# Gate and up of the second feed-forward as seven products of half blocks, with its input scaled in place and the last four output blocks of the merge in one group

## The chip, the cores and the metric

The kernel runs on one core of one Trainium2 chip. The metric is the device time in microseconds (us) of one execution; lower is better. TensorE (PE) does the matmuls and writes to PSUM, which has eight banks. VectorE (DVE), ScalarE (ACT) and GpSimd (POOL) do the work between them, and SyncE (SP) issues nearly all transfers. Each engine takes its instructions in the order in which they stand in its own queue; semaphores tie the queues together.

## What is computed

One step of a hybrid streaming encoder over 1072 rows: 16 meta tokens, 1024 prompt frames, 32 sample frames. The parts that matter here, cut from the reference:

```python
def half_ffn(x, g, w_gate, w_up, w_down):
    h = rmsnorm(x, g)
    return x + 0.5 * ((jax.nn.silu(h @ w_gate) * (h @ w_up)) @ w_down)

x = half_ffn(x, ffn1...)            # first feed-forward, D_MODEL 1024, D_FF 2816
...                                 # projections, attention branch oa, recurrent branch ob
merged = gates[..., :D_MODEL] * (oa @ w_branch_a) + gates[..., D_MODEL:] * (ob @ w_branch_b)
x = x + merged @ w_out
x = half_ffn(x, ffn2...)            # second feed-forward
y = rmsnorm(x, final_norm)
```

The meta rows are not part of the output, so that everything from the merge on runs over 1056 columns.

## The kernel before, in words

Activations lie transposed: model channels on the partitions (8 blocks of 128), rows of the batch along the free axis. Every operand is split into a high part (`h`, rounded to fp32r) and a low part (`l`, the rest); a product of two operands is three matmuls, high by high, high by low, low by high. A split is one ACT copy and one DVE subtraction (`split`, and `weights` for a weight block of 128x1024: `whi` by ACT L184, `wlo` by DVE L185). Three `whi`/`wlo` buffers rotate, and two raw buffers into which SP loads.

The **first feed-forward** cuts the 1072 columns into four blocks of 268 and works in three stages. `first_units(0)` and `first_units(1)` compute the first two of 22 column blocks of gate and up in the plain way: per quarter `q` and matrix 24 matmuls of 268 columns. Between them DVE and ACT form the sums of half blocks `T1` to `T4` (`sums`). Then ten rounds of `unit` for gate and for up compute two column blocks at once with seven products of half blocks (12 matmuls each, for each of two column halves `b`) where the plain way has eight. DVE forms the sums of weights for it (`sa`, `sb`). The middle results go to `mid_dram`. Last, `mid` loads and splits them, and the down products run, 6 matmuls for each of 8 output blocks `m` and three column tiles, added into `acc` by DVE.

The **merge** runs over the column tiles `TD`, which are called A (384 columns from 16), B (384 from 400) and C (288 from 784) below. `merge(m)` makes one of eight blocks of `merged`; `out_block` multiplies two of them by `w_out` and DVE adds the result to `acc` (L1381). The order is merge 0, 1, 2, out(0,1), merge 3, 4, out(2,3), merge 5, 6, out(4,5), merge 7, out(6,7).

The **second feed-forward** (`ffn`) has no sums. `scaled`/`normalise` splits `acc` times the gain into `xh2`, `xl2` as soon as a tile of `acc` is final (ACT L216, DVE L217); this does not need the norm. Beside it the squares are summed over the 8 blocks: five blocks on POOL, three on DVE. `finish` then multiplies the sums by a matrix of ones on PE, and `scale_rows` makes the row factor `R2` from that: three ACT steps and four POOL steps (L249 to L252). `R2` is used only behind the products, in `finish` of `gate_up` (L284, L286). Each of 22 column blocks needs 24 matmuls for each matrix and tile; after every second block, two blocks of down products run. The last two are followed by the final norm (`after2`).

A tile framework puts each engine's instructions into an order of its own when the kernel is built, by its own costs; `PE.on` holds PE to the order in which the code is written.

## Time and profile before

| what | value |
|---|---|
| median of 3 runs | 2548.09 us (2545.7 to 2548.61) |
| the profiled execution | 2547.18 us, its span 2545.4 us |
| PE busy in the span | 2497.2 us (98%) |
| DVE, ACT, POOL busy | 1418.6, 815.5, 247.0 us |
| merge to second feed-forward, 1755 to 1800 us | PE busy 43.08 of 45 us |
| second feed-forward, 1800 to 2540 us | PE busy 735.84 of 740 us |
| units of the first feed-forward, 113 to 505 us | PE busy 392.00 of 392 us |

"Busy" of PE counts overlapping matmuls once. An idle stretch is shown in brackets behind the instruction that ended it, with the engine that released it. A matmul's printed duration (0.34 us) includes its passage through the array; the pace of a stream is the distance from start to start.

### The profile page before, as it was taken

What the parts mean: (1) busy time and instruction counts of PE and PEld (TensorE: products, weight loads), DVE (VectorE), ACT (ScalarE), POOL (GpSimd) and SP (SyncE); (2) the same over time, 40 slices, a digit from 0 to 9 for tenths busy, and PEclk for the clock granted to TensorE, in tenths of its full rate; (3) what the DMA queues carried; (4) which work ended last, traced back from release to release, by engine and by line L of the source; (5) the groups of instructions that cost most, each with busy time, mean ns of one, the idle gap of its engine ahead of it and who ended that gap; (6) DMA issues with size and microseconds to landing.
All of it is one profiled execution on the core that took longest, in us unless ns stands there. A gap on an engine that the chain in (4) does not pass through costs nothing.

```text
span 2545.4 us, 44180 instructions
## 1 busy us (share of the span) xinstructions
PE 2497.2 (98%) x18396; PEld 2397.6 (94%) x18396; DVE 1418.6 (56%) x2635; ACT 815.5 (32%) x1652; POOL 247.0 (10%) x388
## 2 busy tenths in 40 slices
PE   6999999999999999999999999999999999999998
PEld 5999999999998999998888888999999999999998
DVE  4655555577675467764655665557443444444445
ACT  6433333411124233332544543325211111111113
POOL 1000000000003012221000000214111001000100
PEclk9999999999999999999999999999999999999999
DMA  7122222352222111112111214321111111111112
GB/s 200 58 88 68 85 68 90 109 185 84 87 73 90 42 43 55 47 58 59 43 47 43 68 52 150 119 84 42 51 50 38 46 50 50 37 48 50 49 35 77
DMA packets 219182, 179.38 MB, mean 70 GB/s; under 512 B 37270, under 2 KB 202390, under 8 KB 218982
## 3 DMA queue, kind: packets, MB, share of 16 engines
q1 hardware_dynamic: 218950, 176.56, 22.3%
q8 instruction: 144, 2.36, 0.4%
q14 instruction: 56, 0.46, 0.1%
q0 software_dynamic: 32, 0.00, 0.0%
HBM read 137.78 MB, written 38.75 MB: 69 GB/s over the span
## 4 chain that ended last, share of the span: by engine, by line
PE 92%; DVE 5%; ACT 2%; issue 1%; DMA 1%; POOL 0%; SPq 0%; DVEq 0%; ACTq 0%; POOLq 0%
PE ps_z L100 37%; PE ps_mm L100 33%; PE ps_o L100 11%; PE ps_tr L100 8%; PE ps_tr L103 2%; DVE xl L217 1%; PE ps_z L103 1%; DVE wlo L185 1%; ACT whi L184 0%; PE ps_mm L103 0%; DVE left L993 0%; DVE acc L1381 0%; DMA xt<-in_x_prompt_dram 0%; DMA ga<-gate_dram 0%; DVE sd L875 0%
## 5 line engine op out<-in xcount | busy, mean ns | idle before, releaser
L100 PE MATMUL ps_mm<-xh,whi 128*128 128x384 f32 (+2 forms) x1224 | 405.4, 331 | 0.5 <-DVE raw L1201 0.5
L100 PE MATMUL ps_mm<-xh,wlo 128*128 128x384 f32 (+2 forms) x1224 | 399.1, 326 | 0.0
L100 PE MATMUL ps_mm<-xl,whi 128*128 128x384 f32 (+2 forms) x1224 | 398.2, 325 | 0.0
L184 ACT ACTIVATE whi<-raw 128x1024 fp32r<-128x1024 f32 x152 | 158.1, 1056 | 669.5 <-PE ps_z L100 429.4
L100 PEld LDWEIGHTS ps_mm<-xh,whi 128*128 128x128 f32 x1224 | 230.5, 188 | 9.1 <-issue 5.0
L100 PE MATMUL ps_z<-xh,whi 128*128 128x384 f32 (+2 forms) x720 | 234.9, 326 | 4.0 <-ACT whi L184 2.4
L100 PE MATMUL ps_z<-xh,wlo 128*128 128x384 f32 (+2 forms) x720 | 234.0, 325 | 0.1
L100 PE MATMUL ps_z<-xl,whi 128*128 128x384 f32 (+2 forms) x720 | 234.0, 325 | 0.0
L100 PEld LDWEIGHTS ps_mm<-xl,whi 128*128 128x128 f32 x1224 | 230.5, 188 | 1.2
L100 PEld LDWEIGHTS ps_mm<-xh,wlo 128*128 128x128 f32 x1224 | 230.7, 189 | 0.4
L185 DVE TENSOR_TENSOR wlo<-raw,whi 128x1024 fp32r<-128x1024 f32 x152 | 185.8, 1236 | 46.6 <-ACT whi L184 44.1
L100 PEld LDWEIGHTS ps_z<-xh,whi 128*128 128x128 f32 x720 | 136.1, 189 | 5.0 <-ACT whi L184 2.7
L286 POOL TENSOR_TENSOR g<-g,R 128x384 f32<-128x384 f32 (+1 forms) x66 | 77.7, 1178 | 641.4 <-ACT g L116 641.4
L993 DVE TENSOR_TENSOR_SCAN left<-left,oneb 128x512 f32<-128x512 f32 (+6 forms) x112 | 107.3, 958 | 54.8 <-ACT left L116 54.2
L100 PEld LDWEIGHTS ps_z<-xh,wlo 128*128 128x128 f32 x720 | 136.5, 190 | 0.9 <-DVE wlo L185 0.9
L100 PEld LDWEIGHTS ps_z<-xl,whi 128*128 128x128 f32 x720 | 136.2, 189 | 0.2
L287 DVE TENSOR_TENSOR g<-ps_z,g 128x384 f32<-128x384 f32 (+1 forms) x66 | 34.6, 524 | 179.1 <-PE ps_z L100 177.9
L116 ACT ACTIVATE g<-g 128x268 f32<-128x268 f32 (+2 forms) x126 | 58.1, 461 | 192.5 <-DVE g L284 148.3
L100 PE MATMUL ps_z<-ml,whi 128*128 128x384 f32 (+1 forms) x360 | 116.4, 323 | 0.0
L100 PE MATMUL ps_z<-mh,wlo 128*128 128x384 f32 (+1 forms) x360 | 115.8, 322 | 0.0
L100 PE MATMUL ps_z<-mh,whi 128*128 128x384 f32 (+1 forms) x360 | 115.7, 321 | 0.0
L100 PE MATMUL ps_z<-xe,whi 128*128 128x268 f32 (+3 forms) x424 | 111.9, 310 | 0.0
(581 smaller groups left out, 6240.7 us busy)
## 6 DMA issues: line engine op xcount, KB each, us to landing
raw<-in_ffn_w_gate_dram SPq DMA_DIRECT2D x44, 512.0 KB, 3.7
raw<-in_ffn_w_up_dram SPq DMA_DIRECT2D x44, 512.0 KB, 3.6
raw<-in_ffn_w_down_dram SPq DMA_DIRECT2D x44, 512.0 KB, 4.3
raw<-in_w_in_dram SPq DMA_DIRECT2D x44, 512.0 KB, 3.8
mid_dram<-g SPq DMA_DIRECT2D x22, 536.0 KB, 2.7
mid<-mid_dram SPq DMA_DIRECT2D x22, 536.0 KB, 3.7
gate_dram<-gst SPq DMA_DIRECT2D x32, 192.0 KB, 1.9
acc<-x_dram SPq DMA_DIRECT2D x3, 1536.0 KB, 6.7
```

The source lines that it names most:

```text
L100: return self.queue(nc.tensor.matmul(*args, **more))
L103: return self.queue(nc.tensor.transpose(*args, **more))
L116: i = A.activation(out, in_, func, **more).ins
L184: A.activation(hi, raw, AF.Copy)
L185: V.tensor_tensor(lo, raw, hi.bitcast(F32), op=ALU.subtract)
L217: V.scalar_tensor_tensor(xl[:, k, s], srcs[k], g, xh[:, k, s].bitcast(F32), op0=ALU.mult, op1=ALU.subtract)
L286: G.tensor_tensor(g[:, :n], g[:, :n], R[:, s], op=ALU.mult)
L287: V.tensor_tensor(g[:, :n], pu[:, :n], g[:, :n], op=ALU.mult)
L993: V.tensor_tensor_scan(rev(st[:rows]), rev(st[:rows]), one, 1.0 if carry is None else carry[:rows], op0=ALU.mult, op1=ALU.mult)
```

## The change

- The functions of the first feed-forward (`first_units`, `unit`, `hilo`, `mid` and the down loop) move into a class `Seven`. For the first feed-forward the same instructions come out in the same order.
- The second feed-forward uses `Seven` with four blocks of 264 columns (`QW2`), q0 to q3: 16 to 280, 280 to 544, 544 to 808, 808 to 1072. Gate and up of all 22 column blocks come first, 2 plain and 20 in ten rounds of seven products; the middle results go through `mid_dram`; the down products follow.
- The sums need the scaled input. So `normalise` goes: `squares` sums the squares (four blocks on POOL, four on DVE), `finish` makes `R2` and calls `operands`, which multiplies each block of `acc` in place by gain and `R2` (DVE L1370) and splits it into the places that `oh`/`ol` had. What lies behind the products in `finish` of `gate_up` becomes a Silu and a product without `R2`.
- `acc` before scaling is stored to `x2_dram` and loaded back for the down products. `T1` to `T3` take its place in between.
- `out_block` runs for the blocks 4 to 7 in one group of 12 matmuls, with a fourth pair of weight buffers in `raw2` (`spare`). Inside it, behind the fourth output block of tile B and of tile C, PE has the product with ones for the tile ahead. The ones product of tile C stands behind q0 of the first plain block. `PE.on` holds for the out group and the first plain block.
- `gfin` lies in the buffer of `R2`, `yt` in `raw2`.

The diff, cut:

```diff
+QW2 = (T - N_META) // 4
...
-        xh2, xl2 = big("xh", F32R), big("xl", F32R)
-        def scaled(t0, n):
-            if n:
-                finish_one()
-            if behind:
-                normalise(pool, chunks(acc, *behind[0]), xh2, xl2, 2, R2, *behind.pop(0))
-            if n:
-                behind.append((t0, n))
+        ff = Seven(pool, N_META, QW2, ffn2_w_gate, ffn2_w_up,
+                   dict(g=("ml", 4), s=("ga", 2), S=("gb", 2), raw2=("raw2", 2)))
+        def squares(t0, n):
+            tots = []
+            for first, last, eng in ((0, 4, G), (4, KC, V)):
+                tot = temp(pool, "tot")
+                A.activation(tot[:, :n], acc[:, first, t0:t0 + n], AF.Square)
+                for k in range(first + 1, last):
+                    sq = temp(pool, "sq")
+                    A.activation(sq[:, :n], acc[:, k, t0:t0 + n], AF.Square)
+                    eng.tensor_tensor(tot[:, :n], tot[:, :n], sq[:, :n], op=ALU.add)
+                tots.append(tot)
+            def finish():
+                ps = bank(rotate=True)
+                PE.matmul(ps[:, :n], ones, tots[0][:, :n], start=True, stop=False)
+                PE.matmul(ps[:, :n], ones, tots[1][:, :n], start=False, stop=True)
+                scale_rows(pool, ps, R2, t0, n)
+                operands(t0, n)
+            waiting.append(finish)
+        def operands(t0, n):
+            for q in range(4):
+                for c, t, w in pieces(q):
+                    if not t0 <= t < t0 + n:
+                        continue
+                    b, th = divmod(q, 2)
+                    for kh in range(2):
+                        for k in range(4 * kh, 4 * kh + 4):
+                            v = acc[:, k, t:t + w]
+                            V.scalar_tensor_tensor(v, v, gains[:, 2, k:k + 1], R2[:, t:t + w],
+                                                   op0=ALU.mult, op1=ALU.mult)
+                        h, l = B[kh, th, b]
+                        split(h[:, :, c:c + w], l[:, :, c:c + w], acc[:, 4 * kh:4 * kh + 4, t:t + w])
...
         def out_block(cs, mids, last):
-            ws = [weights([(w_out[0][c * P:(c + 1) * P, :], 1)]) for c in cs]
+            ws = [weights([(w_out[0][c * P:(c + 1) * P, :], 1)], spare if x == 3 else None) for x, c in enumerate(cs)]
...
                     for m in range(KC):
                         one(m, t0, n)
-                    scaled(t0, n)
+                        if m % 2:
+                            nc.sync.dma_start(x2_dram[:, m - 1:m + 1, t0:t0 + n], acc[:, m - 1:m + 1, t0:t0 + n])
+                        if m == 3:
+                            finish_one()
+                    squares(t0, n)
...
-            if m % 2 == 0 and m >= 2:
+            if m in (2, 4):
                 out_block((m - 2, m - 1), [mids.pop(m - 2), mids.pop(m - 1)], False)
         functions("natural_log_exp_and_others")
-        out_block((6, 7), [mids.pop(6), mids.pop(7)], True)
+        kept()
+        PE.on = True
+        out_block((4, 5, 6, 7), [mids.pop(m) for m in range(4, KC)], True)
+        ff.plain(0, after=lambda q: finish_one())
+        PE.on, PE.last = False, None
+        t4s = [sums(b) for b in range(2)]
+        ff.plain(1)
+        for b in range(2):
+            X["T4", b] = B[0, 1, b]
+            split(*X["T4", b], t4s[b])
+        ff.rest()
+        acc = big("acc", F32)
+        for t0, n in TD:
+            nc.sync.dma_start(acc[:, :, t0:t0 + n], x2_dram[:, :, t0:t0 + n])
...
-        ffn(pool, TD, acc, xh2, xl2, R2, ffn2_w_gate, ffn2_w_up, ffn2_w_down, None,
-            "sqrt_and_others", after2, opening)
+        ff.down(ffn2_w_down, TD, acc, ((("mh", 4), ("mh", 4)), (("gb", 2), ("gb", 2)),
+                                       (("mh", 4), ("mh", 4)), (("ga", 2), ("ga", 2))),
+                "sqrt_and_others", after2)
```

Up to the second last out group the order of all engines is the same in both kernels. Three places where it is not follow.

DVE, out group, between tile A and the sums of squares of tile B. `acc_17238` is tile A and `acc_17239` tile B in the changed kernel; before, tile B is `acc_17238` and tile C `acc_17239`. `t_tot` before and `t_ga` after are the sums of squares. Before:

```order
L226 TENSOR_TENSOR t_tot<-t_tot,t_sq 128x384
L1381 TENSOR_TENSOR acc_17238<-ps_z,acc_17238 128x384
L217 SCALAR_TENSOR_TENSOR xl_17247<-acc_17238,gains,xh_17244 128x384
L1381 TENSOR_TENSOR acc_17238<-ps_tr,acc_17238 128x384
L217 SCALAR_TENSOR_TENSOR xl_17247<-acc_17238,gains,xh_17244 128x384
```

After:

```order
L1370 SCALAR_TENSOR_TENSOR acc_17238<-acc_17238,gains,R 128x120 x5
L204 TENSOR_TENSOR xl0s<-acc_17238,xh0s 128x1056
L204 TENSOR_TENSOR xl2s<-acc_17238,xh2s 128x4x120
L1370 SCALAR_TENSOR_TENSOR acc_17238<-acc_17238,gains,R 128x120 x3
L1432 TENSOR_TENSOR acc_17239<-ps_z,acc_17239 128x384
L1432 TENSOR_TENSOR acc_17239<-ps_o,acc_17239 128x384
L204 TENSOR_TENSOR xl1s<-acc_17238,xh1s 128x4x120
L1432 TENSOR_TENSOR acc_17239<-ps_z,acc_17239 128x384
L1339 TENSOR_TENSOR t_ga<-t_ga,t_gb 128x384
```

The scaling of tile A, which reads `R`, now stands ahead of the last evacuations of tile B and of its sums of squares.

DVE, last stretch ahead of the weights of the first gate block (`wlo<-raw,whi`, the first of each excerpt). `acc_17240` is tile C after. Before:

```order
L1381 TENSOR_TENSOR acc_17239<-ps_z,acc_17239 128x288
L217 SCALAR_TENSOR_TENSOR xl_17247<-acc_17238,gains,xh_17244 128x384
L1381 TENSOR_TENSOR acc_17239<-ps_o,acc_17239 128x288
L217 SCALAR_TENSOR_TENSOR xl_17248<-acc_17239,gains,xh_17245 128x288
L185 TENSOR_TENSOR wlo<-raw,whi 128x1024
```

After:

```order
L1370 SCALAR_TENSOR_TENSOR acc_17239<-acc_17239,gains,R 128x144 x7
L204 TENSOR_TENSOR xl2s<-acc_17239,xh2s 128x4x144
L1370 SCALAR_TENSOR_TENSOR acc_17239<-acc_17239,gains,R 128x144
L1370 SCALAR_TENSOR_TENSOR acc_17239<-acc_17239,gains,R 128x240 x5
L204 TENSOR_TENSOR xl1s<-acc_17239,xh1s 128x4x144
...
L1432 TENSOR_TENSOR acc_17240<-ps_z,acc_17240 128x288
L1432 TENSOR_TENSOR acc_17240<-ps_mm,acc_17240 128x288
L1339 TENSOR_TENSOR t_ga<-t_ga,t_gb 128x288
L204 TENSOR_TENSOR xl1s<-acc_17239,xh1s 128x4x240
L1339 TENSOR_TENSOR t_ga<-t_ga,t_gb 128x288
L187 TENSOR_TENSOR wlo<-raw,whi 128x1024
```

The whole scaling of tile B now stands ahead of these weights.

PE, the border from the merge to the second feed-forward. Before:

```order
L100 MATMUL ps_o<-mh,wlo 128x288
L100 MATMUL ps_z<-t_tot,cst 128x384 x2
L100 MATMUL ps_mm<-xh_17243,whi 128x384
L100 MATMUL ps_mm<-xl_17246,whi 128x384
L100 MATMUL ps_mm<-xh_17243,wlo 128x384
```

After:

```order
L102 MATMUL ps_mm<-mh,spare_18544 128x288
L102 MATMUL ps_mm<-ml,spare_18544 128x288
L102 MATMUL ps_mm<-mh,spare_18545 128x288
L102 MATMUL ps_z<-xh0s,whi 128x264
L102 MATMUL ps_z<-xl0s,whi 128x264
L102 MATMUL ps_z<-xh0s,wlo 128x264
```

The ones product of tile A no longer stands at the border, and the third matmul of the block reads the low part of the first gate weights in both.

## Rows read from the trace of the kernel before

**Rows 1.** The page: busy time of each engine; the chain that ended last.

```profile
PE 2497.2 (98%) x18396; PEld 2397.6 (94%) x18396; DVE 1418.6 (56%) x2635; ACT 815.5 (32%) x1652; POOL 247.0 (10%) x388
PE 92%; DVE 5%; ACT 2%; issue 1%; DMA 1%; POOL 0%; SPq 0%; DVEq 0%; ACTq 0%; POOLq 0%
```

**Rows 2.** Busy time by stage: length, engines (instructions), clock, DMA share, GB/s.

```profile
113.00:505.00 392.00, 392.00 (x3176) 392.00 (x3175) 207.84 (x336) 148.85 (x270) 0.00 (x0) 1.00 0.25 80
505.00:775.00 270.00, 268.50 (x1644) 264.54 (x1642) 197.92 (x334) 59.72 (x81) 9.99 (x8) 1.00 0.34 113
1755.00:1800.00 45.00, 43.08 (x249) 40.80 (x249) 24.95 (x35) 25.45 (x45) 24.27 (x25) 1.00 0.16 48
1800.00:2540.00 740.00, 735.84 (x4600) 734.85 (x4598) 315.39 (x542) 135.53 (x230) 73.36 (x62) 1.00 0.16 47
```

**Rows 3.** Chain, second feed-forward: start, length, 24 matmuls of 288 and of 384.

```profile
1782.72 3.20 PE ps_z L100 x24
1790.14 4.22 PE ps_z L100 x24
```

**Rows 4.** PE in order of time at the border: start, duration, instruction, idle ahead.

```profile
1756.26 1.45 PE L100 MATMUL ps_z<-t_tot,cst 128*128 128x384 f32 x4
1757.26 0.63 PE L100 MATMUL ps_mm<-xh,whi 128*128 128x384 f32 x1
```

**Rows 5.** DVE in order of time at the border, and in the first feed-forward's sums.

```profile
1756.47 0.60 DVE L217 SCALAR_TENSOR_TENSOR xl<-acc,gains,xh 128x384 fp32r<-128x384 f32 x1
1757.00 0.45 DVE L1381 TENSOR_TENSOR acc<-ps_o,acc 128x288 f32<-128x288 f32 x1
1757.36 0.50 DVE L217 SCALAR_TENSOR_TENSOR xl<-acc,gains,xh 128x288 fp32r<-128x288 f32 x1
1757.79 1.21 DVE L185 TENSOR_TENSOR wlo<-raw,whi 128x1024 fp32r<-128x1024 f32 x1
1758.92 7.23 DVE L217 SCALAR_TENSOR_TENSOR xl<-acc,gains,xh 128x288 fp32r<-128x288 f32 x6
...
84.39 1.27 DVE L202 TENSOR_TENSOR xe<-S,acc1s 128x1072 fp32r<-128x1072 f32 x1
85.58 0.43 DVE L502 TENSOR_TENSOR g<-ps_z,g 128x268 f32<-128x268 f32 x1
```

**Rows 6.** ACT in order of time at the border: weights, row factor.

```profile
1756.66 1.04 ACT L184 ACTIVATE whi<-raw 128x1024 fp32r<-128x1024 f32 x1
1772.17 0.56 ACT L246 ACTIVATE ms<-ps_mm,epsb 128x384 f32<-128x384 f32 x1
1774.47 0.52 ACT L116 ACTIVATE ys<-ys 128x384 f32<-128x384 f32 x1
```

**Rows 7.** POOL in order of time at the border: sums of squares, row factor.

```profile
1758.19 5.26 POOL L226 TENSOR_TENSOR t_tot<-t_tot,t_sq 128x384 f32<-128x384 f32 x4 [14.03 <-ACT t_tot L222]
1775.07 1.01 POOL L249 TENSOR_TENSOR ms<-ms,ys 128x384 f32<-128x384 f32 x1 [1.52 <-ACT ys L116]
1777.87 1.02 POOL L252 TENSOR_TENSOR R<-ys,ms 128x384 f32<-128x384 f32 x1
```

**Rows 8.** Border behind the first feed-forward: stages as in rows 2, PE in time.

```profile
782.00:784.00 2.00, 0.37 (x2) 0.37 (x3) 2.00 (x3) 2.00 (x4) 1.92 (x3) 1.00 0.00 0
786.00:788.00 2.00, 1.74 (x3) 0.92 (x4) 2.00 (x3) 0.00 (x0) 1.92 (x2) 0.50 0.00 0
790.00:792.00 2.00, 2.00 (x8) 1.98 (x8) 0.00 (x0) 1.73 (x2) 1.81 (x3) 0.53 0.75 206
...
788.08 0.54 PE L100 MATMUL ps_z<-xh,whi 128*128 128x400 f32 x1
788.41 0.54 PE L100 MATMUL ps_z<-xl,whi 128*128 128x400 f32 x1
```

**Rows 9.** Page, transfers: size, median us from issue to landing.

```profile
raw<-in_ffn_w_gate_dram SPq DMA_DIRECT2D x44, 512.0 KB, 3.7
```

**Rows 10.** DVE, first evacuation of the first feed-forward's down products.

```profile
513.65 0.57 DVE L633 SCALAR_TENSOR_TENSOR acc<-ps_tr,acc 128x400 f32<-128x400 f32 x1 [0.68 <-DMA acc<-x_dram]
```

More of the change, by code (lines that the diff above doesn't have):

```diff
@@ L330, in tile_encoder_step @@
     x0_dram = dram.tile([P, KC, T], F32, name="x0_dram")
+    x2_dram = dram.tile([P, KC, T], F32, name="x2_dram")
     mid_dram = dram.tile([FC, P, T], F32, name="mid_dram")
@@ L1390, in out_block, with spare @@
                         one(m, t0, n)
+        def spare():
+            return [pool.tile([P, D], F32R, tag="raw2", name=f"spare{x}", bufs=2) for x in range(2)]
         mids = {}
```

395 lines of the change are left out of this document (198 added, 197 removed).

## Prediction

> **What bounds the kernel now.** I began with the page. PE is busy for 98% of the span and holds 92% of the chain that ended last [rows 1]. The table by stage then says where that is so: the second feed-forward's stage has 735.84 busy in 740 us, and the border ahead of it 43.08 in 45 [rows 2]. There is next to no idle time to win there, so the change can gain only by giving PE less to do. The first feed-forward already runs the code that the change brings: in its units PE was busy 392.00 of 392 us, while DVE needed 207.84 (53%), ACT 148.85 and POOL nothing [rows 2]. So the sums of weights hide behind PE in that code, and PE time that is removed from gate and up is time gained. What is new is the border: there the input was ready without the row factor, and now it isn't.
>
> **What is removed from PE.** Before, gate and up take 22 column blocks x 2 matrices x 8 blocks of input x 3 products x 3 tiles = 3168 matmuls, 2112 of 384 columns and 1056 of 288. In the chain 24 of 384 take 4.22 us, 175.8 ns each, and 24 of 288 take 3.20 us, 133.3 ns [rows 3]. That is 371.4 + 140.8 = 512.2 us. After, two plain blocks take 2 x 2 x 4 x 24 = 384 matmuls and the ten rounds 10 x 2 x 7 x 2 x 12 = 3360, together 3744 of 264 columns. The first feed-forward's 268 columns took 392.00/3176 = 123.4 ns [rows 2]; scaled by 264/268 that is 121.6 ns, and 455.3 us. Scaling down from 288 by the slope of rows 3 (0.443 ns a column) gives 122.7 ns, 459.3 us, as the dear end; I take 121.6, since its row has the nearest shape. **Gain 56.9 us**, at least 52.9. The down products (1584 matmuls) stay, and the out group has as many matmuls as the two groups that it replaces.
>
> The two paces of rows 3 lie 0.443 ns a column apart, so that a matmul has a fixed price of only 133.3 - 288 x 0.443 = 6 ns, and splitting work into matmuls of fewer columns costs little. The Trainium skill ("TensorE: Matmul & The Clock Gate", section "Back-to-back issue gap") speaks against the change here: it gives about 81 ns a matmul in a sustained stream at 128 columns and 131 at 512, most of it a fixed price. Read between these as a straight line, that is an estimated 114, 102 and 99 ns at 384, 288 and 264 columns, 349 us before and 370 after: gate and up would lose 21 us. The trace disagrees: 384 columns take 175.8 ns [rows 3], more than the page has for 512.
>
> **What the border costs.** I set t = 0 where the out group begins tile B. Without waits it would run 16 output blocks, eight of 2.11 us (12 x 175.8) and eight of 1.60, and two products with ones. Such a product (two matmuls in plain f32) took 1757.26 - 1756.26 = 1.0 us [rows 4]. That is 31.7 us. The steps against it:
>
> 1. Row factor of A. Its ones product ends at 9.4. ACT needs 0.56 and twice about 0.52 [rows 6]. POOL first finishes sums of squares of tile B (5.26/4 = 1.3 us each, three of them) and then needs four steps, from 1775.07 to 1777.87 + 1.02, 3.8 us [rows 7]. R2 of A is there at about 17.
>
> 2. DVE's block for A. The order puts 16 scalings, two splits and one evacuation of A and B in front of tile B's last evacuations and sums. From start to start a scaling-like operation took 0.53 us at 384 columns (1756.47 to 1757.00) and 0.43 at 288 (1757.36 to 1757.79) [rows 5]; by that slope 0.41 at 264, 0.38 at 240, 0.28 at 144 and 0.26 at 120. A split of 1072 elements took 85.58 - 84.39 = 1.19 [rows 5], 1.17 for 1056. The block is 8 x 0.41 + 8 x 0.26 + 2 x 1.17 + 0.56 = 8.3 us, until 25.3, and the evacuations and sums of B behind it need some 4 more, until 29.5. PE stands at tile B's ones product from 24.3: **it waits 5.2 us**, and the out group ends at 29.5 + 1.0 + 6.4 = 36.9.
>
> 3. DVE's block for B. R2 of B comes 7.5 us behind that product's end at 30.5, at 38.0 (three sums of tile C and 3.8 us on POOL, as in step 1). Then DVE has 8 x 0.28 + 8 x 0.38 + 2 x 0.66 + 1.06 = 7.7 us of scaling and splits (0.66 is 1.17 scaled to 576 elements), 2.5 of evacuations, sums and a last split, and only then the low weights of the first gate block, 1758.92 - 1757.79 = 1.13 us [rows 5]. They are ready at 49.4. Two matmuls of that block need only the high part; the third needs this one. Without waits it would start at 31.9. **The loss is 17.5 us with the 5.2 of step 2 in it**, so that some 12 us of it lie in the first gate block. Everything that DVE owes PE stands behind these low weights in its queue. The high part doesn't come early either: the group of four holds all three buffers until its end, and its ACT copy takes 1.04 [rows 6].
>
> 4. The clock. Behind the first feed-forward PE had 0.37 us of work in the 2 us from 782; from 786 on the granted clock was 0.50 (the 1.2 GHz level), and at 788.08 two matmuls of 400 columns lay 0.33 us apart; at 790 to 792 it was 0.53 [rows 8]. At full speed 400 columns are 183 ns by the slope of rows 3. About 4.3 us at that pace lose **2 us**. I count it once, behind the 12 us; a fall behind the 5.2 is paid for by the wait that follows.
>
> 5. Small waits. The first plain block's q2 needs tile C, whose ones product stands behind q0: 1.0 us. The low weights of the second plain block stand behind sums in DVE's queue: 1.3. At the start of the out group the weights of merge 7's buffers come free only when merge 7 ends, and 1.04 + 1.13 of weight work [rows 5, 6] stand against 1.05 us of matmuls: 1.2. Together **3.5 us**, each between 0 and 3. Weights take 3.7 us from issue to landing [rows 9], well inside the border, and the transfers of `acc` to `x2_dram` have nobody waiting.
>
> 6. Start of the down products. In the first feed-forward the first evacuation waited 0.68 us for the reloaded `acc` [rows 10]. Here the reload starts some 3.5 us later. Eight banks of PSUM, each filled in 6 x 175.8 ns = 1.05 us, cover 8 us of that: nothing. Without that cover it would be 3 us.
>
> 7. The norm at the end has one buffer more or less for its result: nothing, up to 0.3.
>
> Steps 3 to 5 make 17.5 + 2 + 3.5 = 23.0. The old border had 45 - 43.08 = 1.9 us idle [rows 2], which goes: **21.1 us**. With this the change gives -56.9 + 21.1 = -35.8, and 2547.18 - 35.8 = 2511.4 for the profiled execution. That one lies 0.9 below the median of the runs: **2512 us**.
>
> **The rivals.** A. *The border is mostly hidden.* If R2 comes some microseconds earlier (POOL's sums for B behind the four steps and not ahead, or scalings at less than 0.41 us), step 2 vanishes and step 3 shrinks to some 5 to 9 us; the time is then 2494 to 2503. Against it stands the length of DVE's queue, which the order fixes: 10 us of scaling and evacuating for B lie ahead of the weights in any case.
>
> B. *The border is dearer.* Beside POOL's sums at 1758.19 to 1763.45 [rows 7], six operations of DVE took 7.23 us, 1.2 each in place of 0.43 [rows 5]. If the scalings meet POOL in the same way, 32 of them cost up to 0.8 us more, 25 us in all, and every one stands on the path. But POOL works then only for parts of these blocks: half of that is 12 us, and the time 2524, at the full price 2537. The trace speaks for the mechanism; against it, POOL's sums are mostly over when R2, POOL's own last step, arrives.
>
> C. *Slower, by the clock.* The waits could leave PE at 1.2 GHz for long, if the small waits of step 5 keep it from rising again. At 0.5 a matmul of 264 columns costs about 0.1 us more (0.33 against 0.183 at 400, scaled). The 35.8 us are gone after some 360 matmuls, and if the two plain blocks and the first round (384 + 336) all ran so, 72 us would be lost: 2584. Against it: in rows 8 the fall lasted some 6 us with the stream running again.
>
> D. *The smaller matmuls bring nothing.* The change has 3744 matmuls in place of 3168. If a matmul had a large fixed price, so that one of 264 columns took 136.8 ns (512.2 us in all), gate and up would gain nothing, and the border alone would show: 2569. The row for 268 columns, 123.4 ns over 3176 of them [rows 2], all but excludes that: 0.01. The page's rule above would be this rival.
>
> **How the numbers follow.** My forecast, the border at 12 to 32 us (2503 to 2523): 0.62. A, below 2503: 0.14. B, 2523 to 2542: 0.18. C: 0.02. D: 0.01. Something unnamed that ends within 0.2%: 0.03. 0.2% is 5.1 us, about what a measurement of this kernel can tell from no change. The range for 8 in 10 takes the forecast's own and the nearer part of A and B: 2500 to 2527; the dear end of the pace, 4 us more, lies in it. Faster 0.94, same 0.03, slower 0.03.
>
> **What would show it.** In the profile of the changed kernel: units of the second feed-forward without idle time, at 121.6 ns a matmul (step of the gain); PE idle for about 5 us ahead of tile B's ones product, released by DVE's sums at L1339 (step 2); about 12 us idle inside the first gate block, released by DVE's `wlo` at L187 (step 3); a granted clock of 0.5 for some microseconds behind it (step 4); waits of 1 us at q2 and at the second plain block (step 5); no idle time at the first down products (step 6). A border without the 12 us, scalings at L1370 of over 0.8 us, or a pace above 123 ns would make the prediction wrong.

## The result and the profile after

The changed kernel takes 2515.08 us (median of 4 runs, 2513.43 to 2515.86) against 2548.35 before (4 runs): 0.987 of the time, 95% interval 0.9858 to 0.9882, 33.3 us faster. The forecast was 2512, its range 2500 to 2527. The profiled execution took 2515.86 us with a span of 2514.1, 31.3 less than the span before.

The page of the changed kernel: busy time of each engine, and the chain that ended last (as in [rows 1]).

```profile
PE 2454.2 (98%) x18972; PEld 2349.2 (93%) x18972; DVE 1530.4 (61%) x2826; ACT 889.4 (35%) x1783; POOL 162.8 (6%) x319
PE 90%; DVE 5%; ACT 2%; issue 1%; POOL 1%; DMA 1%; SPq 0%; DVEq 0%; POOLq 0%; ACTq 0%
```

PE has 576 more matmuls and 43 us less to do; DVE has 112 us more. Busy time by stage (columns as in [rows 2]): the end of tile B in the out group, the border, and the units.

```profile
1720.00:1754.00 34.00, 34.00 (x203) 33.47 (x203) 14.54 (x30) 10.01 (x17) 8.60 (x9) 1.00 0.16 59
1754.00:1766.00 12.00, 7.98 (x37) 6.76 (x36) 6.62 (x17) 5.56 (x12) 5.03 (x7) 0.72 0.31 115
1766.00:1780.00 14.00, 4.95 (x31) 4.50 (x30) 13.31 (x29) 6.27 (x9) 0.85 (x1) 0.69 0.39 122
1780.00:1800.00 20.00, 18.86 (x143) 18.23 (x143) 16.34 (x34) 10.47 (x15) 3.47 (x4) 0.96 0.30 90
1840.00:2250.00 410.00, 410.00 (x3347) 409.83 (x3346) 222.07 (x362) 153.47 (x278) 0.00 (x0) 1.00 0.29 93
```

The units run without a gap, with DVE at 54%, as the first feed-forward did. Of what is idle, 13.1 us lie between 1754 and 1780, and some 3 us in small waits ahead of and behind that. Here are PE's waits from 1700 to 1860 us (for whom: total, times, longest):

```profile
PE ps_z L102 <- DVE wlo L187: 9.8, 3, 8.1
PE ps_tr L102 <- DVE t_ga L1339: 4.0, 1, 4.0
PE ps_z L102 <- ACT whi L186: 0.9, 1, 0.9
PE ps_o L102 <- ACT xh0s L203: 0.7, 1, 0.7
PE ps_o L102 <- DVE xl0s L204: 0.5, 1, 0.5
```

PE in order of time at the border (start, duration, instruction, idle time ahead); tile B begins at 1729.86:

```profile
1729.86 0.34 PE L102 MATMUL ps_z<-mh,whi 128*128 128x384 f32 x1
...
1759.22 1.65 PE L102 MATMUL ps_tr<-t_ga,cst 128*128 128x384 f32 x2 [4.02 <-DVE t_ga L1339]
...
1778.44 0.59 PE L102 MATMUL ps_z<-xh0s,wlo 128*128 128x264 f32 x1 [8.12 <-DVE wlo L187]
1778.83 0.42 PE L102 MATMUL ps_z<-xh0s,whi 128*128 128x264 f32 x1
1779.05 0.42 PE L102 MATMUL ps_z<-xl0s,whi 128*128 128x264 f32 x1
```

The ones product of tile B waits for DVE's sums of squares, and the third matmul of the first gate block for the low gate weights. Behind it the matmuls stand 0.22 us apart, and the granted clock of the stretch around them is 0.69: PE has dropped to the 1.2 GHz level. DVE and POOL show why (B's sums, then the two row factors, the scaling of A and B, the low weights):

```profile
1746.77 2.92 DVE L1370 SCALAR_TENSOR_TENSOR acc<-acc,gains,R 128x264 f32<-128x264 f32 x7 [4.32 <-POOL R L254]
1758.62 0.55 DVE L1339 TENSOR_TENSOR t_ga<-t_ga,t_gb 128x384 f32<-128x384 f32 x1
1766.88 2.05 DVE L1370 SCALAR_TENSOR_TENSOR acc<-acc,gains,R 128x144 f32<-128x144 f32 x7 [0.69 <-POOL R L254]
1777.17 1.22 DVE L187 TENSOR_TENSOR wlo<-raw,whi 128x1024 fp32r<-128x1024 f32 x1
```

```profile
1745.71 1.02 POOL L254 TENSOR_TENSOR R<-ys,ms 128x384 f32<-128x384 f32 x1
1759.31 1.69 POOL L1339 TENSOR_TENSOR t_ga<-t_ga,t_gb 128x288 f32<-128x288 f32 x2 [12.58 <-ACT t_gb L1338]
1762.31 0.80 POOL L1339 TENSOR_TENSOR t_ga<-t_ga,t_gb 128x288 f32<-128x288 f32 x1 [1.31 <-ACT ys L118]
1765.84 1.01 POOL L254 TENSOR_TENSOR R<-ys,ms 128x384 f32<-128x384 f32 x1
```

DVE starts to scale a tile as soon as POOL has written its row factor, and does nothing but this tile's scalings and splits until the last scaling.

Where the 31.3 us of the two spans went, term by term:

| term | predicted | measured | from |
|---|---|---|---|
| gate and up, products | -56.9 | -56.4 | before 22 blocks of 23.24 us (chain, from the group at 1790.14 to its like at 1813.38), 511.3; after 3744 matmuls 121.5 ns apart, 454.9 (the 3360 of the units run from 1830.33 to 2238.59) |
| third matmul of the first gate block | +17.5 | +16.7 | 1778.44 - 1729.86 = 48.6 against 31.9 without waits |
| low clock behind that wait | +2 | +1.5 | 13 matmuls in 3.03 us (1778.44 to 1781.47) in place of 1.58 |
| small waits | +3.5 | +2.9 | 0.65 at the start of the out group, 0.66 + 0.49 at q2, 1.07 at the second up block |
| idle time of the old border | -1.9 | -1.9 | [rows 2] |
| down products and the final norm | 0 | +3.9 | ten pairs of column blocks in 233.85 us (2238.59 to 2472.44) in place of 10 x 23.04; the last pair to the end of the span 41.65 in place of 41.18 |
| start of the merge, not touched by the change | 0 | +2.7 | a wait of 2.86 in place of 1.68 us, then a granted clock of 0.58 (1587 to 1591), worth 1.5 us |
| ahead of the merge, not touched | 0 | -1.0 | that wait began 1.0 us earlier |

The sum is -31.6, within 0.3 us of the difference of the spans. The two rows on parts that the change doesn't touch are scatter: in another run of the same kernel (after_again) that wait was 2.2 us without a fall of the clock.

### The profile page after: what moved, and what is told of

The parts are those of the page before. It is cut to its first block, busy times and chain, and to the rows that moved or that the text cites. A ratio compares the mean times of both kernels' runs of the same rounds, so it can differ in the third digit from the quotient of the medians.

```text
span 2514.1 us, 46009 instructions
## 1 busy us (share of the span) xinstructions
PE 2454.2 (98%) x18972; PEld 2349.2 (93%) x18972; DVE 1530.4 (61%) x2826; ACT 889.4 (35%) x1783; POOL 162.8 (6%) x319
## 4 chain that ended last, share of the span: by engine, by line
PE 90%; DVE 5%; ACT 2%; issue 1%; POOL 1%; DMA 1%; SPq 0%; DVEq 0%; POOLq 0%; ACTq 0%
PE ps_z L102 36%; PE ps_mm L102 33%; PE ps_o L102 10%; PE ps_tr L102 8%; PE ps_tr L105 2%; PE ps_z L105 1%; DVE wlo L187 1%; DVE acc L1370 1%; DVE xl L219 1%; PE ps_mm L105 0%; ACT whi L186 0%; DVE left L957 0%; DMA ga<-gate_dram 0%; DVE sd L839 0%; DMA xt<-in_x_prompt_dram 0%
## 5 line engine op out<-in xcount | busy, mean ns | idle before, releaser
L102 PE MATMUL ps_mm<-xh,whi 128*128 128x384 f32 (+2 forms) x960 | 319.4, 333 | 0.6 <-DVE raw L1165 0.6
L102 PE MATMUL ps_mm<-xh,wlo 128*128 128x384 f32 (+2 forms) x960 | 313.0, 326 | 0.0
L102 PE MATMUL ps_mm<-xl,whi 128*128 128x384 f32 (+2 forms) x960 | 312.5, 326 | 0.0
L437 DVE SCALAR_TENSOR_TENSOR acc<-ps_z,acc 128x384 f32<-128x384 f32 (+2 forms) x264 | 138.8, 526 | 72.5 <-PE ps_z L102 71.0
L203 ACT ACTIVATE whi<-S 128x1024 fp32r<-128x1024 f32 x80 | 85.0, 1062 | 155.9 <-PE ps_z L102 145.2
L204 DVE TENSOR_TENSOR wlo<-S,whi 128x1024 fp32r<-128x1024 f32 x80 | 97.9, 1224 | 30.2 <-ACT whi L203 28.9
L102 PE MATMUL ps_z<-acc1s,whi 128*128 128x268 f32 (+1 forms) x480 | 106.0, 285 | 0.0
L102 PE MATMUL ps_z<-xl1s,whi 128*128 128x268 f32 (+1 forms) x368 | 105.1, 286 | 0.0
L102 PE MATMUL ps_z<-xh1s,wlo 128*128 128x268 f32 (+1 forms) x368 | 104.9, 285 | 0.0
L102 PE MATMUL ps_z<-xh1s,whi 128*128 128x268 f32 (+1 forms) x368 | 104.6, 284 | 0.0
```

What stands on the lines that cost most here:

```text
L102: return self.queue(nc.tensor.matmul(*args, **more))
L203: A.activation(dst_h, src, AF.Copy)
L204: V.tensor_tensor(dst_l, src, dst_h.bitcast(F32), op=ALU.subtract)
L437: V.scalar_tensor_tensor(acc[:, m, s], ps[:, :n], 0.5, acc[:, m, s], op0=ALU.mult, op1=ALU.add)
```

## The experiments

Each is compared with the changed kernel; "before" in a ratio is the kernel before on the same chip. "To the down products" is the time in the trace from the end of the wait at the start of the merge to the first down product, which leaves out the scatter ahead of that point: 651.5 us in the changed kernel, 650.4 in after_again. Most of the 1.1 us between these two is the low clock at the start of the merge, which the measure still holds. It fell in the changed kernel, all_plain, early_gate, warm, unlocked and mid_pairs_m, and cost each 1.3 to 1.6 us; these are compared with 651.5. In the other runs it stayed at 1.00 there; these are compared with 650.4. The medians of the changed kernel in its two runs lie 1.5 us apart (2515.08 and 2513.62), so smaller differences of medians say nothing.

**all_plain: the units undone.**

```diff
-        for b in range(2):
-            X["T4", b] = B[0, 1, b]
-            split(*X["T4", b], t4s[b])
...
-        ff.rest()
+        for c in range(2, FC):
+            ff.plain(c)
```

> The border, the sums and the down products stay as in the changed kernel; all 22 column blocks of the second feed-forward's gate and up run in the plain way, so that the 3360 matmuls of the units become 3840. My theory: the gain of the change lies in the count of matmuls alone, at 121.7 ns each. 480 more cost 58.4 us: 2515.1 + 58.4 = 2573.5 us, which is 25 us slower than before; that would be the price of the border and of all else that isn't a unit. Rival (a part of the gain comes from something else, as smaller tiles or the middle results' way through DRAM): the difference to the changed kernel is under 50 us or over 65.

Measured: 2573.52 us, 1.0101 of before (1.0086 to 1.0116). The difference to the changed kernel is 58.4 us, 121.7 ns for each of the 480 matmuls, as expected. That it agrees to the tenth is partly luck, since the intervals of the two ratios leave some 4 us, but the traces give 58.2 as well (709.7 and 651.5 us to the down products). The whole gain lies in the count of matmuls; without the units the new border and the rest would cost 25.6 us. This also prices a matmul of 264 columns: by the straight line through the two sustained figures of the Trainium skill ("TensorE: Matmul & The Clock Gate", section "Back-to-back issue gap"), an estimated 99 ns at 264 columns, it would have been 47.5 us. This stream doesn't follow them.

**two_groups: blocks 4, 5 and 6, 7 again in two groups.**

```diff
-            if m in (2, 4):
+            if m in (2, 4, 6):
...
-        out_block((4, 5, 6, 7), [mids.pop(m) for m in range(4, KC)], True)
+        out_block((6, 7), [mids.pop(m) for m in (6, 7)], True)
```

> Undoes one part: the output blocks 4, 5 and 6, 7 of the merge again run as two groups, with the ones products in the last of them. My theory: the chain row factor of A, DVE's block, ones product of B, row factor of B, DVE's block, low gate weights is what sets the start of the first gate block; PE's output blocks only run beside it. Tile B and C then give 14.9 us less of PE work beside a chain that shortens only by 4.2 us (the ones product of A comes 4.2 us earlier). So the wait ahead of B's ones product grows to some 12 us, the one in the first gate block stays, and the kernel is 9 to 12 us slower than the changed one: 2524 to 2527. Rival (the border is bound by weights and buffers, not by the chain): within 3 us of the changed kernel.

Measured: 2517.04 us, 0.9882 of before (0.9867 to 0.9897); 653.1 us to the down products, 2.7 more. The expectation of 9 to 12 us fell. PE's waits at the border:

```profile
PE ps_tr L102 <- DVE t_ga L1339: 10.1, 1, 10.1
PE ps_mm L102 <- DVE wlo L187: 7.6, 1, 7.6
```

The wait at B's ones product did grow, to 10.1 us. But the one at the low gate weights is gone: `ps_mm` is the up block. A group of two leaves the third pair of weight buffers free, the gate weights are split early, and the next thing in DVE's queue is late instead. Counted from the start of the merge, A's ones product came 8.6 us later than in after_again (158.9 and 150.3 us), the third matmul of the first up block only 0.8 us (195.9 and 195.1). So the group of four wins 8.6 us as cover and gives nearly all of them back; that it holds all weight buffers until its end is the reason for a part of this, since behind B's row factor that matmul came after 9.8 us here and 16.0 in the changed kernel.

**early_gate: buffers of their own for the first gate weights.**

```diff
+                gw0.append(weights([(ffn2_w_gate[0][:, :P], KC)], early))
                 for t0, n in TD:
...
+        def early():
+            return [pool.tile([P, D], F32R, tag="ga", name=f"early{x}", bufs=2) for x in range(2)]
...
-        ff.plain(0, after=lambda q: finish_one())
+        ff.plain(0, after=lambda q: finish_one(), gw=gw0[0])
```

> The weights of the first gate block get two buffers of their own (those of the merge's gates, with the sums of squares packed into others), and are loaded and split at the start of the out group, ahead of the scaling of tile B in DVE's queue. The waits of 0.93 and 8.12 us in the first gate block go. My theory: DVE's queue as a whole is late, so the next thing in it, the low weights of the first up block, is late next, at about the same time as the low gate weights were; only the 2.9 us of the first gate products move ahead of the wait, with up to 1.4 us of them back at full clock: 3 to 4.5 us faster than the changed kernel, 2510.5 to 2512, with a wait of 5 to 6 us on the up block's low weights. Rival (this one split was the whole delay): 8 to 10 us faster, no wait behind it.

Measured: 2514.43 us, 0.987 of before (0.9855 to 0.9885); 653.4 us to the down products, 1.9 more. PE's waits at the border:

```profile
PE ps_mm L102 <- DVE wlo L187: 7.0, 1, 7.0
PE ps_tr L102 <- DVE t_gb L1339: 5.6, 1, 5.6
PE ps_z L102 <- ACT whi L186: 2.9, 1, 2.9
```

The up block's low weights are late next, as expected, 7.0 us. The 2.9 were not expected: ACT's order took the early weights ahead of the out group's own. The third matmul of the out group came 3.0 us later from the start of the merge than in the changed kernel (130.2 and 127.2 us; the 2.2 us of the expectation for unlocked are too few), the clock fell behind that wait (0.72 from 1716 to 1722), and A's ones product came 4.4 us later (155.6 and 151.2 us). This hides what the edit won, and neither the 3 to 4.5 us of the theory nor the 8 to 10 of the rival came.

**late_q1: tile A's last 120 columns behind B's sums.**

```diff
-                operands(t0, n)
+                if t0 == TD[0][0]:
+                    operands(t0, n, (0,))
+                    later.append(lambda: operands(t0, n, (1,)))
+                else:
+                    operands(t0, n)
...
                     squares(t0, n)
+                    if later:
+                        later.pop()()
```

> The scaling and splits of tile A's last 120 columns (they belong to q1, which PE needs last) are issued behind tile B's evacuations and sums of squares; nothing else changes. My theory: these 8 scalings and two splits, 3 to 3.5 us, are most of the 4.0 us that PE waits for B's ones product, and since B's row factor and everything behind it follow from that product, the whole chain moves ahead: 3 to 4.5 us faster than the changed kernel, 2510.5 to 2512, the wait ahead of B's ones product under 1.2 us, the one in the first gate block about as long as before. Rival (the wait in the first gate block takes up what is gained, since the low gate weights hang on something else than the chain): within 1 us of the changed kernel.

Measured: 2513.93 us, 0.9868 of before (0.9852 to 0.9884); 649.7 us to the down products, 0.7 less, about what the rival foretold. The wait at B's ones product fell from 4.02 to 0.63 us, as expected. The chain behind it did not follow. ACT in order of time behind that product, which ran from 1753.94 to about 1755:

```profile
1756.02 0.61 ACT L203 ACTIVATE xh1s<-acc 128x480 fp32r<-128x480 f32 x1 [0.98 <-DVE acc L1374]
1756.53 0.43 ACT L1335 ACTIVATE t_ga<-acc 128x288 f32<-128x288 f32 x1
1756.87 0.43 ACT L1338 ACTIVATE t_gb<-acc 128x288 f32<-128x288 f32 x1
1757.20 0.56 ACT L248 ACTIVATE ms<-ps_tr,epsb 128x384 f32<-128x384 f32 x1
```

The first step of the row factor, `ms`, stands in ACT's queue behind a split of tile A that waits for DVE, and behind two squares. It began some 2.2 us after its input was there, so that B's row factor came 1.0 us earlier and not 3.4. The time that PE won at the ones product it then waited ahead of the first gate block: 5.7 us for ACT's `whi`, and 7.8 for `wlo`, about as before.

**m_outer, mid_pairs, mid_pairs_m: the pace of the down products.** A pair of column blocks, from its first matmul to that of the next stage, took 1855.28 - 1832.24 = 23.04 us before and 2285.30 - 2261.86 = 23.44 after:

```profile
1832.24 0.34 PE L100 MATMUL ps_tr<-mh,whi 128*128 128x384 f32 x1
...
1855.28 0.34 PE L100 MATMUL ps_tr<-xh,whi 128*128 128x384 f32 x1
```

```profile
2261.86 0.34 PE L102 MATMUL ps_mm<-mid_mh,whi 128*128 128x384 f32 x1
...
2285.30 0.51 PE L102 MATMUL ps_mm<-mid_mh,whi 128*128 128x384 f32 x2
```

The expectations below take 23.27 us for a pair after the change. That is the first pair alone; the nine behind it took 23.36 to 23.45, so that ten pairs lose 3.5 us, not 2.2. The three runs did not find the cause, but the trace of the changed kernel shows most of it, not in PE's waits but in those of its weight loads from 2200 to 2480 us (before, there were none from 1800 to 2480):

```profile
PEld ps_mm L102 <- ACT whi L186: 2.5, 10, 0.3
```

```profile
2286.08 0.30 PEld L102 LDWEIGHTS ps_mm<-mid_gb,whi 128*128 128x128 f32 x2 [0.24 <-ACT whi L186]
```

```profile
2284.97 2.01 ACT L186 ACTIVATE whi<-raw 128x1024 fp32r<-128x1024 f32 x2 [19.45 <-PE ps_z L102]
```

Before, gate and up lay between two pairs. Now pair follows pair, each reads two of the three rotating weight buffers until its end, and the weights of the next pair's second block can be split only when PE lets go of one. ACT's first copy at 2284.97 ends at about the time when PE can load, four matmuls into the pair. With a smaller delay at the low weights the matmuls there come 0.24 us late in each pair. No run has a fourth buffer; of the 3.5 us about 1 is left without a cause.

m_outer:

```diff
-                for t0, n in tiles:
-                    for m in range(KC):
+                    for m in range(KC):
+                        for t0, n in tiles:
+                            one(m, t0, n)
```

> In nine of the eleven pairs of the second feed-forward's down products the loops change places: output block outside, column tile inside, as before the change; the first and the last pair stay. Nothing else. In the trace a pair of column blocks (144 matmuls) took 23.05 us before the change (2.88 us for the three tiles of an output block) and 23.27 after it, in which the tile is outside. Theory: the order of the loops is the cause of these 0.22 us, so that nine pairs go back to 23.05 and the kernel is 2.0 us faster than the changed one, 2513. Rival (the operands, whose low and high parts lie in other buffers now, or their alignment): 23.27 us stay and the time with them, 2515.

Measured: 2515.14 us, 0.9873 of before (0.9858 to 0.9888). From the first to the last down product 263.6 us, in the changed kernel 263.4, and the ten waits of the weight loads are there as in the changed kernel. The order of the loops is not the cause.

mid_pairs (mid_pairs_m has both edits):

```diff
-                raw = self.tile("g", [P, T])
+                raw = self.pool.tile([P, T], F32, tag="ga", name="g", bufs=2) if self.t0 else self.tile("g", [P, T])
...
-        ff.down(ffn2_w_down, TD, acc, ((("mh", 4), ("mh", 4)), (("gb", 2), ("gb", 2)),
-                                       (("mh", 4), ("mh", 4)), (("ga", 2), ("ga", 2))),
+        ff.down(ffn2_w_down, TD, acc, ((("mh", 4), ("ml", 4)),) * 4,
```

> The middle results that the second feed-forward's down products read are split into the pairs of buffers that they had before the change (high part in one tag, low part in the other), in the place of two buffers of one tag; the order of the loops stays as changed. m_outer showed that the order alone does not bring back the 0.22 us a pair of column blocks. Theory: where the operands lie decides the pace; a pair takes 23.05 us again, 2.4 us less over eleven pairs, 2512.7. Rival (neither by itself): 23.27 us stay, 2515.

> Both together: the pairs of buffers as before the change and, in nine of eleven pairs, output block outside and column tile inside. If either of them decides by itself, this is as fast as that one; if both are needed, only this one takes 23.05 us a pair of column blocks (2.0 us less in all, 2513); if the cause lies elsewhere, 23.27 us stay here too, 2515.

Measured: 2529.74 us, 0.9937 of before (0.9922 to 0.9952), and 2530.12 us, 0.9936 (0.9921 to 0.9951), 14.7 and 15.0 slower than the changed kernel. One wait makes most of it, here in mid_pairs at the first down product:

```profile
2248.00 0.69 PE L102 MATMUL ps_mm<-mid_mh,whi 128*128 128x384 f32 x1 [11.72 <-ACT mid_mh L203]
```

The edit took the raw middle results into buffers that the last units still held, and so laid bare what hides the start of the down products: that the first middle results can be loaded and split while the last unit runs. From the first to the last down product they took 267.7 and 267.8 us, slower by 4 us and not faster. 3.3 and 2.9 of these are the first pair (26.5 and 26.2 us), which began at the low clock (0.50 from 2248 to 2252 in mid_pairs); the pairs behind it took 23.4 to 23.7. Both theories fell. In mid_pairs nine of the waits for `whi` were still there, 2.1 us.

**warm: matmuls to no purpose in the two waits.**

```diff
+                if t0 == TD[1][0]:
+                    fill[-1](26)
                 ps = bank(rotate=True)
                 PE.matmul(ps[:, :n], ones, tots[0][:, :n], start=True, stop=False)
...
                     squares(t0, n)
+                busy(60)
```

> PE gets matmuls of 288 columns into a bank that nobody reads, 26 ahead of B's ones product (3.5 us of a wait of 4.0) and 60 ahead of the first gate block (8.0 us of waits of 9.0); they are shorter than the waits, so that they delay nothing. Theory: behind both waits the matmuls ran at the 1.2 GHz level for some microseconds; without that, B's ones product takes 1.0 us rather than 1.7, which moves B's row factor and all behind it by 0.7, and the first 14 products of the gate block are 1.4 us shorter. 2.1 us faster than the changed kernel, 2513, the granted clock 1.0 from 1754 to 1782 us. Rival (the clock costs nothing there, since waits take up what it loses): within 0.7 us of the changed kernel.

Measured: 2514.36 us, 0.987 of before (0.9854 to 0.9887); 652.9 us to the down products, 1.4 more. PE's busy time and granted clock (columns: stretch, length, busy, clock, DMA share, GB/s):

```profile
1758.00:1762.00 4.00, 3.42 (x21) 1.00 0.65 240
1780.00:1782.00 2.00, 2.00 (x11) 0.50 0.57 150
1784.00:1786.00 2.00, 2.00 (x13) 0.66 0.47 141
```

In the first wait the clock held, and B's ones product took 0.9 us in place of 1.65. It brought nothing: the row factor came 7.6 us after that product's start as before, since POOL's three sums of tile C (2.57 us) stood ahead of its four steps and hid the difference. So a fall of the clock behind the first wait is paid for by the next wait, as the prediction had it. The second filling ended too soon: the output blocks ran at full clock, PE reached it earlier, and 3.7 us of waiting were left. Behind these the clock fell all the same, for 25 matmuls some 0.22 us apart, more than the 13 behind 8.1 us of waiting. The run doesn't price the second fall; it shows that a filling which stops short of the wait's end buys nothing.

**unlocked: four moves at once.**

```diff
+                    if t0 == TD[1][0]:
+                        gw0.append(weights([(ffn2_w_gate[0][:, :P], KC)], early, last_sq[0]))
...
-                operands(t0, n)
+                if later:
+                    later.pop()()
+                if t0 == TD[0][0]:
+                    operands(t0, n, (0,))
+                    later.append(lambda: operands(t0, n, (1,)))
+                elif t0 == TD[1][0]:
+                    operands(t0, n, (1,))
+                    later.append(lambda: operands(t0, n, (2,)))
...
+            mid()
             for q in range(4):
```

> Four moves at the border, none of which changes what is computed. The first gate block's weights have buffers of their own and are split behind tile A's squares, not ahead of the out group's own weights. The scaling of tile A's last 120 columns is issued behind B's ones product and row factor, and no longer ahead of B's sums. Tile B is scaled in two parts, q1's 144 columns first, then the low weights of the first up block, then q2's 240 columns. My theory after late_q1 and early_gate: three queues hold the chain, and each edit alone only handed the wait on. In late_q1 B's ones product came 3.4 us earlier, but ACT's first step of the row factor stood behind a split of tile A that waited for DVE, so that R2 came only 1.0 us earlier; in early_gate ACT took the early weights ahead of the out group's, which began 2.2 us later. With all of them out of the way the wait at B's ones product is under 1 us, the gate block starts without a wait at about the end of the out group, and waits of 1 to 3 us remain at the up block's low weights and at q2: 8 to 14 us faster than the changed kernel, 2501 to 2507. Rival (DVE's work as a whole, some 45 us of scaling, splits and sums between the out group and the first unit, is the bound): what is gained at the gate block comes back as waits in the second plain block or the first unit, 2509 to 2514.

Measured: 2520.53 us, 0.9894 of before (0.9879 to 0.9909), 5.5 slower than the changed kernel; 656.5 us to the down products. The third matmul of the first up block came some 9.6 us earlier than in the changed kernel, but:

```profile
PE ps_mm L102 <- DVE wlo L189: 11.4, 2, 7.8
PE ps_o L102 <- ACT xh0s L205: 2.5, 1, 2.5
```

3.7 of the 11.4 us are the first up block, 7.8 the second: its low weights stood at 1808.24 in DVE's queue, behind all sums for the units, and the first unit's weights behind them. The rival had foretold that the waits come back, but with 2509 to 2514 it was out too, as was the theory with 2501 to 2507. Whether it is the amount of DVE's work or its order was still open.

**unlocked2: the second plain block's weights ahead of the sums, POOL's sums of C behind B's row factor.**

```diff
+        w1 = [weights([(w[0][:, P:2 * P], KC)]) for w in (ffn2_w_gate, ffn2_w_up)]
         t4s = [sums(b) for b in range(2)]
-        ff.plain(1)
+        ff.plain(1, gw=w1[0], uw=w1[1])
...
+                    if eng is G and t0 == TD[2][0]:
+                        tc.add_manual_dep(made.ins, last_R[0].name, order, reason="order")
```

> As unlocked, with two more moves. The weights of the second plain block are issued ahead of the sums for the units, so that DVE splits them ahead of most sums (in unlocked PE waited 7.76 us for the low weights of the second up block, which stood behind all sums). POOL's three sums of squares of tile C are held behind the four steps of B's row factor (in the changed kernel they take 2.6 us ahead of these steps). My theory: DVE's and POOL's orders, not the amount of their work, are what sets the border: up block 0 starts 10 us earlier as in unlocked, R2 of B comes up to 2.5 us earlier still, and no wait of over 2 us is left in the second plain block: 4 to 10 us faster than the changed kernel, 2505 to 2511. Rival (DVE's amount of work between the out group and the first unit is the bound, whatever the order): the waits come back in the first unit, within 2 us of the changed kernel, 2513 to 2517, or slower.

Measured: 2506.23 us (2504.77 to 2508.08), 0.9844 of before (0.9828 to 0.9861), 8.9 faster than the changed kernel by the medians, some 6.6 by the two ratios to before, and the fastest full computation here; 642.6 us to the down products, 7.8 less. PE's waits at the border:

```profile
PE ps_mm L102 <- DVE wlo L189: 2.9, 1, 2.9
PE ps_tr L102 <- DVE t_gb L1346: 2.3, 1, 2.3
PE ps_mm L102 <- ACT whi L186: 1.9, 1, 1.9
PE ps_o L102 <- ACT xh0s L205: 1.8, 1, 1.8
PE ps_z L102 <- DVE wlo L189: 0.9, 1, 0.9
```

9.8 us of waits are left of 15.9, no engine has less work than in the changed kernel, and the second block's weights are early. So order, not amount, set at least these 7 to 9 us of the border. One part of the expectation failed: with POOL's sums out of the way B's row factor still came 7.9 us after B's ones product began, because now ACT's steps ahead of POOL's were late. POOL's sums then met DVE's scaling instead:

```profile
1762.48 3.94 DVE L1388 SCALAR_TENSOR_TENSOR acc<-acc,gains,R 128x144 f32<-128x144 f32 x8 [3.35 <-POOL R L258]
```

Eight of 144 columns in 3.94 us are 0.49 each, with POOL at its sums for 2.4 us of these; in the changed kernel they took 0.28.

**no_factor and after_again: nothing waits for the row factor.**

```diff
-                            V.scalar_tensor_tensor(v, v, gains[:, 2, k:k + 1], R2[:, t:t + w],
+                            V.scalar_tensor_tensor(v, v, gains[:, 2, k:k + 1], R1[:, :w],
...
+        R1 = pool.tile([P, QW2], F32, tag="r1", name="r1", bufs=1)
+        V.memset(R1, 1.0)
```

> The scaling of the second feed-forward's input takes a tile of ones in the place of the row factor, so that this part of the norm is left out; squares, ones products, row factor, scaling, splits and sums all run as often as before, but nothing waits for the row factor. It prices that wait by itself. My theory: the chain through the row factor makes nearly all of the border's loss; without it DVE scales each block as soon as it is final, the wait in the first gate block falls from 9 to under 3 us, and 12 to 17 us go: 2498 to 2503. Rival (DVE's amount of work at the border is the bound, factor or not): 2508 or more.

> The changed kernel once more, on the chip of no_factor, to compare with. Both theories: 2515 us, the waits of 4.0 us ahead of B's ones product and of 8.1 at the low gate weights again; the wait at the start of the merge, which is no part of the change, may differ by a microsecond either way.

Measured: 2505.21 us, 0.9835 of before (0.9818 to 0.9851), and 2513.62 us for the changed kernel once more, 0.9867 (0.9853 to 0.9882). Taking the row factor's wait away wins 8.4 us, 8.7 in the traces (641.8 and 650.4 us to the down products), and not 12 to 17. This is no clean price of the factor: without the dependency the framework also put DVE's queue in another order, DVE was busy for 1537.0 us in place of 1528.7, as its scalings now met POOL's sums, and a wait for the high gate weights took the place of the old ones. How the rest of the border's loss divides between the factor and the order in the queues stays open. PE's waits that are left, then DVE at one place, and what POOL did there:

```profile
PE ps_z L102 <- ACT whi L186: 5.2, 1, 5.2
PE ps_z L102 <- DVE wlo L187: 1.7, 2, 1.1
```

```profile
1736.96 2.42 DVE L1373 SCALAR_TENSOR_TENSOR acc<-acc,gains,r 128x144 f32<-128x144 f32 x2
1739.30 0.55 DVE L1435 TENSOR_TENSOR acc<-ps_tr,acc 128x384 f32<-128x384 f32 x1
1739.77 3.52 DVE L1373 SCALAR_TENSOR_TENSOR acc<-acc,gains,r 128x144 f32<-128x144 f32 x4
```

```profile
1737.00 3.25 POOL L1342 TENSOR_TENSOR t_ga<-t_ga,t_gb 128x384 f32<-128x384 f32 x3 [14.32 <-ACT t_ga L1338]
```

PE now waits 5.2 us for the high gate weights. And here the scaling ran beside POOL's sums: 1.2 us each for 144 columns at 1736.96, four times the 0.28 of the changed kernel, while an evacuation from PSUM between them kept its 0.55. The Trainium skill ("SBUF — State Buffer", section "Who interferes with whom") has it that a DVE instruction with two inputs in SBUF contends with a GpSimd instruction that reads SBUF; the evacuation has one input in SBUF, and the trace agrees.

## Why the prediction was right

**What bounds, and the gain.** That PE time removed from gate and up is time gained held: the units have no idle time, and their matmuls came 121.5 ns apart against 121.6 forecast. all_plain, in which PE differs by their count, confirms it. The gain came out at 56.4 and not 56.9, because 4.22 us for 24 matmuls was the longest of its kind; a block of the kernel before took 23.24 us, not 23.28.

**Steps 1 to 3, the chain at the border.** Counted from tile B's start at 1729.86, A's row factor was due at 17 and came at 16.9 (1745.71 + 1.02); B's ones product was due at 29.5 and came at 29.4; B's row factor 38.0, came 37.0; the low gate weights 49.4, came 48.5. The wait of 5.2 us was 4.0, because it began 1.0 later: the matmul behind A's ones product took 0.3 longer, and the first half of B's ones product ran ahead of the wait. So the chain was right in its places, and it was right that it is a chain of queues. One place came out well by luck: from the end of B's ones product to B's row factor it took 6.0 us and not 7.5, because two of POOL's three sums of C were done or under way by then, while the ones product itself, at the low clock, took 1.65 and not 1.0. What the prediction did not say is what each link is worth alone: my first experiments took single links away and won at most 1 us, because ACT's, DVE's and POOL's queues handed the wait on.

**Step 4, the clock.** One fall of 1.5 us behind the long wait, not 2; the fall behind the first wait cost nothing (warm).

**Step 5, small waits.** 2.9 of 3.5: q2 1.15 for 1.0, the second up block 1.07 for 1.3, the start of the out group 0.65 for 1.2.

**Step 6, start of the down products.** No idle time, as forecast. I had named the reload of `acc` and PSUM's banks as its cover. mid_pairs shows another that I had not named: with the raw middle results in buffers that the last units still hold, PE waited 11.7 us. What the named cover is worth no run shows.

**The step that failed** is a line of the gain: "The down products (1584 matmuls) stay". Their count does, but from the first of them to the end the kernel took 3.9 us longer, 3.5 of it in the ten pairs ahead of the last. Some 2.4 us are the short waits at the start of each pair for the weights of its second block, since no gate and up lies between two pairs any more; the rest stays open. With 1.7 us of scatter ahead of and in the merge and 0.5 of gain too few, less 1.9 us by which the waits of the border and the clock were sized too dear, this makes 4.2 of the 4.5 us between the 2511.4 forecast for the profiled execution and its 2515.86.

**The rivals.** A (border mostly hidden) did not happen by itself; unlocked2 shows that 7 to 9 us of it can be had. Its 2494 to 2503 don't all follow from its terms: with 5 to 9 us in place of 17.5 it is 2499.5 to 2503.5, and for 2494 the clock's 2 and the small waits' 3.5 have to go too. B's mechanism is real (no_factor: 1.2 us a scaling beside POOL), but in the changed kernel POOL was through before each scaling began, as its row factor is POOL's last step. C: the clock rose again after 3 us. D is excluded by all_plain.

## What to carry to other kernels

Work that used to run behind the products and now must run ahead of them costs what the queues make of it: write down, for each engine that the chain passes, what stands in its queue in front of the next link, weights and other tiles' work included. Taking one link out of such a chain often shows nothing, because the next queue hands the wait on; here six moves together won 7 to 9 us, where single ones had won about 1 at most and four had lost 5. And an edit that holds all buffers of a rotation for longer (the group of four) should be charged for the load that can't start meanwhile; so should an edit that takes away the work between two users of the rotation, as here between the pairs of down products. Such a wait can be missing in the waits of the matmuls and stand in those of the weight loads.

## What was not expected of the hardware

DVE's scaling of 144 columns took 0.28 us alone, 0.49 on the mean of eight that ran partly beside POOL's sums of 288 columns, and 1.2 beside POOL's sums of 384. A wait of 0.24 us in PE's weight loads, ten times, is most of what looked like a slower pace of the same 144 down matmuls (23.04 and 23.4 us). And the length of a wait alone did not decide on the clock: behind waits of 2.1 to 2.3 us at the start of the merge it stayed at 1.00 in after_again, two_groups and no_factor, and fell to 0.5 in early_gate (2.2 us) and mid_pairs_m (2.1 us); the 1.2 GHz level then lasted for 25 matmuls of 264 columns behind 3.7 us of waiting in warm, but for 13 behind 8.1 us in the changed kernel.
